# Attention on one core: half 0's scaling on VectorE, the sinks' exponentials in two instructions, weights' rests on GpSimd

## The chip, the core and the metric

The kernel runs on one core of one Trainium2 chip. The metric is the device time of one execution in microseconds; each kernel is run several times and the median counts. The engines are TensorE (PE; its weight loads are listed apart as PEld), VectorE (DVE), ScalarE (ACT), GpSimd (POOL) and SyncE (SP), which only issues transfers. Each engine takes its own instructions in the order in which they are written, and semaphores make it wait for the others.

## The reference

The reference is a two-layer decoder trunk in float32 with model width 1024, 512 positions and batch 1. Layer 0 is a gated short convolution, layer 1 is sliding-window attention; each is followed by a SwiGLU of inner width 2816, and every part has an RMSNorm before it and one behind it. The change lies in the attention, whose core is:

```python
kk, vv = with_prev(k), with_prev(v)          # each block of 128 keys with the block before it
scores = einsum('bnqhgd,bnkhd->bnhgqk', qb, kk) * scale
scores = where(valid, scores, NEG)           # window of 128 positions
sink = broadcast_to(sinks, ...)              # one extra logit per head
probs = softmax(concatenate([scores, sink], -1), -1)[..., :-1]
out = einsum('bnhgqk,bnkhd->bnqhgd', probs, vv)
attn = out.reshape(b, s, 1024) @ w_o
```

There are 16 query heads of width 64, 4 heads of keys and values, 4 blocks of 128 positions, and a rotation (rope) of 16 of each head's 64 columns. A head's sink only adds exp(sink − maximum) to the denominator of its softmax.

## The kernel before, in words

**Precision.** Every product of float32 matrices is made of three matmuls on split operands: a high part (the value rounded to the fast format `fp32r`) and a rest (value less high part), multiplied high by rest, high by high and rest by high. So each weight tile that is loaded (`raw`) is first split: ScalarE copies it to `whi`, then VectorE subtracts `wlo = raw - whi`. `split_weights` does this (lines 175 to 190), in one piece of 1024 columns (lines 188 and 189) or, with `slots=True`, in two of 512 (lines 182 and 183).

**The attention loop.** Lines 1542 to 1601 walk ten passes i = 0 to 9. In each they go through the string `ORDER` (lines 47 to 49) token by token, and each token writes the instructions of one step. A round works on one pair of heads (t = i, eight pairs); a token with "-" and the tokens T, P, L, W, O and o work on the pair of the pass before. Since every engine takes its instructions as written, `ORDER` fixes each engine's queue. The steps, each a method of `Heads`, `Queries` or `Early`:

- S: scores on TensorE (line 1334) into the banks `psc`. Half 0 holds the blocks 0 and 1, half 1 the blocks 2 and 3. M: masking and (negated) row maxima `nm` on VectorE (line 1346).
- E: exponentials on ScalarE with their row sums `rs` (line 1361), in four steps, E00 to E11: half, block. Behind the second step of each half stand two small activations for the sinks' exponentials `se` of this half (line 1368), one per head, of two columns.
- N: N0 adds `se` and `rs` (line 1374), takes the reciprocal `rd` (line 1376), both on VectorE, and scales half 0's exponentials on ScalarE, four activations (line 1381); N1 scales half 1's on VectorE, four operations (line 1384). The first block of the sequence has no block before it, so half 0's first piece has 128 columns and the other pieces have 256.
- T: the scaled exponentials are transposed on TensorE into a bank `pt` (line 1396), T0 to T3 by blocks of keys. P and L: the transpose is split, high part `phi` on ScalarE (line 1409), rest `plo` on VectorE (line 1413). W: TensorE weighs the values with both into `po` (line 1422). T2 and T3 use the banks of T0 and T1, so they wait for L0 and L1.
- O: the two halves of the heads' sums are joined, by a copy on ScalarE (line 1431) and an addition on VectorE (line 1433). o: the joined output is split for the output product (lines 1441 and 1442).
- Q, R, H: the queries two pairs ahead are projected on TensorE, rotated (VectorE lines 1261 and 1263, GpSimd lines 1267 and 1270) and split (ScalarE line 1280, then their rest on GpSimd, line 1281, tile `rhl`); the scores of the next round need `rhl`.
- G: weights: in passes 0 to 4 the query weights of the pair three ahead are split, from pass 5 on four tiles of output weights (`rest_w`, j = 0 to 3). g: output weights that are needed early (`early_w`), j = 0 and 1 in pass 4, j = 2 and 3 in pass 6.
- Z (also written Y) and z: parts of the output product that can already be made, in the later rounds.

GpSimd has another task: the SwiGLU weights are combined into sums in memory by transfers that accumulate, and GpSimd's queue issues them (line 547), in every pass behind its steps R and H.

The engines' queues depend on one another in a circle: N needs the exponentials, those need the scores, and those need the queries' split; T needs N.

Of the kernel before, what the change touches and what calls it, by code (L numbers as in the profile page):

```python
# [10 lines left out]
F32 = mybir.dt.float32  # L11
# [33 lines left out]

EARLY_IN, REST_IN = 2, 0
ORDER = (
    "R- S0 T0 T1 Q0 M0 O- Q1 Z0 P0 P1 S1 T2 T3 L0 o- Y0 Q2 L1 G M1 E00 E01 k H- g0 Q3 P2 P3 E10 E11 Z1 z0 W0 L2 L3 A A A N0 W1 W2 N1 W3 g1 z1"
)
NEXT = (0,)  # L50
STEP = {
    "S": "scores", "M": "maxima", "E": "exponents", "N": "normalise", "T": "turn", "P": "high",
    "L": "low", "W": "weigh", "O": "join", "o": "out", "Q": "project", "R": "rotate", "H": "split",
    "G": "weights", "Z": "project", "z": "out",
}
N_SLOT, N_WIDE, N_RAW, N_W = 35, 18, 7, 4
BOTH = 4
# [17 lines left out]
def yoco_kernel(  # L75
# [96 lines left out]
            h = at[1].start // S  # L172
            return self.of[h][:, at[1].start - h * S : at[1].stop - h * S]

    def split_weights(src, raw=None, slots=False):
        if raw is None:
            raw = fetch(src)
        if slots:
            hi, lo = Two("whi", F32R), Two("wlo", F32R)
            for h in range(2):  # L180
                c = slice(h * S, (h + 1) * S)
                nc.scalar.activation(hi[:, c], raw[:, c], AF.Copy)
                nc.vector.tensor_tensor(out=lo[:, c], in0=raw[:, c], in1=hi[:, c].bitcast(F32),
                                        op=ALU.subtract)
# [3 lines left out]
        nc.scalar.activation(hi, raw, AF.Copy)  # L188
        nc.vector.tensor_tensor(out=lo, in0=raw, in1=hi.bitcast(F32), op=ALU.subtract)
        return hi, lo  # L190

    def mm3(out, whi, wlo, xhi, xlo, start, stop, **kw):
# [1092 lines left out]
    class Queries:  # L1285
# [21 lines left out]
    class Heads:  # L1307
# [29 lines left out]
        def maxima(self, half):  # L1337

            pss = self.pss[half]
            nm = small.tile([P, 2, 2], F32, tag="nm", name=name("nm"))  # L1340
            pe = [slot("s") for _ in range(2)]
            self.pe[half], self.nm[half] = pe, nm
            for i, cc in self.spans(half):
                for e in range(2):
                    h = 2 * self.t + e
                    nc.vector.tensor_tensor_reduce(
                        out=pe[e][:, cc], in0=pss[e][:, cc],
                        in1=mask[:, 256 - (cc.stop - cc.start) :],
                        scale=-0.125, scalar=nsnk[:, h : h + 1], op0=ALU.add, op1=ALU.min,
                        accum_out=nm[:, e, i : i + 1],  # L1350
                    )

        def exponents(self, half, i):
            pe, nm = self.pe[half], self.nm[half]
            if half == i == 0:
                self.sums = [small.tile([P, 2, 2, 2], F32, tag=s, name=name(s))
                             for s in ("se", "rs")]
            se, rs = (x[:, half] for x in self.sums)
            cc = self.spans(half)[i][1]
            for e in range(2):  # L1360
                nc.scalar.activation(
                    pe[e][:, cc], pe[e][:, cc], AF.Exp, bias=nm[:, e, i : i + 1],
                    scale=-1.0, accum_out=rs[:, e, i : i + 1],
                )
            if i == 1:
                for e in range(2):
                    h = 2 * self.t + e
                    nc.scalar.activation(se[:, e], nm[:, e], AF.Exp, bias=snk[:, h : h + 1])

        def normalise(self, half):  # L1370
            pe = self.pe[half]
            if half == 0:
                se, rs = self.sums
                nc.vector.tensor_tensor(out=se, in0=se, in1=rs, op=ALU.add)
                self.rd = small.tile([P, 2, 2, 2], F32, tag="rd", name=name("rd"))
                nc.vector.reciprocal(out=self.rd, in_=se)
            rd = self.rd[:, half]
            for i, cc in self.spans(half):
                for e in range(2):
                    if half == 0:  # L1380
                        nc.scalar.activation(pe[e][:, cc], pe[e][:, cc], AF.Copy,
                                             scale=rd[:, e, i : i + 1])
                        continue
                    nc.vector.tensor_scalar(
                        out=pe[e][:, cc], in0=pe[e][:, cc], scalar1=rd[:, e, i : i + 1],
                        scalar2=None, op0=ALU.mult,
                    )
# [154 lines left out]
    with tc.manual_schedule(engines=ALL):  # L1542
        sum_on("a0")
        for i in range(KT + 2):
# [9 lines left out]
            for c in order.split():  # L1554
# [21 lines left out]
                if op in "SMENTPLWOo":  # L1576
                    t -= op in "TPLWOo"
                    of = hp
                elif op in "QRH":
# [118 lines left out]
```

## Time and profile before

| | |
|---|---|
| median of 3 runs | 1028.84 us (1028.47 to 1029.13) |
| the profiled execution | 1030.66 us |
| its span, first to last instruction | 1028.9 us |
| mean granted TensorE clock | 0.997 of full speed |
| busy TensorE / its weight loads | 1007.9 us (98%) / 886.4 us (86%) |
| busy VectorE | 868.9 us (84%) |
| busy ScalarE | 601.9 us (58%) |
| busy GpSimd | 189.6 us (18%) |
| read from HBM | 237.15 MB |

The page of the profile gives the busy time, the span in 40 slices and the groups of instructions; the trace behind it answers for any stretch. A row of a timeline has the start, the duration, the engine, the line, the operation and its tiles (out<-in, partitions x elements), how many like it follow each other without a break, and in square brackets the idle time of the engine ahead of it with what ended it. A row of a list of waits has the engine's instruction, what it waited for, the sum of these waits in us, their number and the mean. A row of a table by windows has the window, its length, and the busy time with the count of instructions of PE, PEld, VectorE, ScalarE and GpSimd, then the granted clock, the share of the transfers' engines and GB/s. A row of a group ends in: busy us, mean ns of one | idle time before them, and what ended most of it.

### The profile page before, as it was taken

To read this page: it belongs to the slowest core of one execution; us is meant where nothing else is said; L and a number is where in the kernel's file an instruction comes from. 1 tells how busy PE (TensorE), PEld (TensorE's weight loads), DVE (VectorE), ACT (ScalarE), POOL (GpSimd) and SP (SyncE) were. 2 spreads that over 40 slices of the span, in tenths; PEclk is the share of its full clock that TensorE was granted. 3 is DMA by queue.
4 is the path that set the end of the run, shared out by engine and by line. 5 is a ranking of instruction groups with operands and counts; after the bars stand their busy time and mean duration, and the time that the engine had idled before them with its cause. 6 is when DMAs were issued, how large, how long until landed. Compare 5 with 4: busy or idle time off the path is not lost. (4 is left out here: it accounts for less than half of the span.)

```text
span 1028.9 us, 16145 instructions
## 1 busy us (share of the span) xinstructions
PE 1007.9 (98%) x5944; PEld 886.4 (86%) x5944; DVE 868.9 (84%) x1448; ACT 601.9 (58%) x1083; POOL 189.6 (18%) x251
## 2 busy tenths in 40 slices
PE   9999999999999999999999989899999999999997
PEld 8888888999889898998897767689998998989986
DVE  5766767899779989989879887878997899899896
ACT  6323445866655464656577877968665563645641
POOL 0433033111111111100114553221211010111001
PEclk9999999999999999999999999999999999999999
DMA  9897689459969699779405887975899666988742
GB/s 357 284 268 223 182 255 351 132 169 292 349 220 301 202 306 339 217 232 327 146 22 155 202 264 172 279 259 146 249 295 324 176 253 210 289 299 255 256 165 82
DMA packets 66575, 244.50 MB, mean 238 GB/s; under 512 B 7872, under 2 KB 8384, under 8 KB 54720
## 3 DMA queue, kind: packets, MB, share of 16 engines
q1 hardware_dynamic: 51328, 145.98, 38.2%
q0 software_dynamic: 14592, 96.48, 37.2%
q8 instruction: 47, 0.77, 0.3%
q10 hardware_dynamic: 576, 1.02, 0.3%
q14 instruction: 32, 0.26, 0.1%
HBM read 237.15 MB, written 102.76 MB: 330 GB/s over the span
## 5 line engine op out<-in xcount | busy, mean ns | idle before, releaser
L479 DVE TENSOR_TENSOR wlo<-raw,whi 128x1024 fp32r<-128x1024 f32 x225 | 274.8, 1225 | 55.6 <-ACT whi L478 55.5
L478 ACT ACTIVATE whi<-raw 128x1024 fp32r<-128x1024 f32 x225 | 233.6, 1050 | 102.0 <-DVE raw L466 29.7
L1072 PE MATMUL gx<-xt,whi 128*128 128x512 f32 x480 | 120.4, 393 | 0.0
L1072 PEld LDWEIGHTS gx<-xt,whi 128*128 128x128 f32 x480 | 86.3, 189 | 15.5
L547 POOL DMA_DIRECT2D hsum<-in_w_gb_dram x96 | 62.5, 729 | 150.8 <-ACT whi L478 89.7
L1034 DVE TENSOR_TENSOR st<-gx,st 128x256 f32<-128x256 f32 x200 | 77.9, 419 | 2.5 <-ACT st L1050 0.4
L1050 ACT ACTIVATE st<-gx 128x256 f32<-128x256 f32 x120 | 43.3, 380 | 62.1 <-PE gx L1075 58.5
L547 POOL DMA_DIRECT2D hsum<-hsum x32 | 25.3, 790 | 293.1 <-ACT whi L478 201.8
L1075 PEld LDWEIGHTS gx<-xt,wlo 128*128 128x128 f32 x480 | 65.5, 190 | 4.7
L1075 PE MATMUL gx<-xt,wlo 128*128 128x256 f32 x480 | 66.9, 282 | 0.0
L1086 ACT ACTIVATE gr<-gr 128x1024 f32<-128x1024 f32 x20 | 21.3, 1063 | 49.9 <-DVE gr L1034 49.9
L193 PE MATMUL px<-wlo,ahi 128*128 128x512 f32 x120 | 46.8, 390 | 1.5 <-DVE mix L648 1.5
L195 PE MATMUL px<-whi,alo 128*128 128x512 f32 x120 | 46.7, 389 | 0.0
L194 PE MATMUL px<-whi,ahi 128*128 128x512 f32 x120 | 46.7, 389 | 0.0
L195 PE MATMUL gz<-xhi,wlo 128*128 128x256 f32 x160 | 45.5, 284 | 0.0
L193 PE MATMUL gz<-xt,whi 128*128 128x256 f32 x160 | 45.3, 283 | 0.0
L194 PE MATMUL gy<-xhi,whi 128*128 128x256 f32 x160 | 45.3, 283 | 0.0
L195 PE MATMUL gy<-xhi,wlo 128*128 128x256 f32 x160 | 45.3, 283 | 0.0
L193 PE MATMUL gy<-xlo,whi 128*128 128x256 f32 x160 | 45.3, 283 | 0.0
L194 PE MATMUL gz<-xt,whi 128*128 128x256 f32 x160 | 45.3, 283 | 0.0
L193 PE MATMUL gz<-xlo,whi 128*128 128x256 f32 x160 | 45.3, 283 | 0.0
L194 PE MATMUL gz<-xhi,whi 128*128 128x256 f32 x160 | 45.3, 283 | 0.0
(294 smaller groups left out, 2965.9 us busy)
## 6 DMA issues: line engine op xcount, KB each, us to landing
hsum<-in_w_gb_dram POOLq DMA_DIRECT2D x96, 512.0 KB, 7.5
raw<-hsum SPq DMA_DIRECT2D x88, 512.0 KB, 7.8
raw<-in_w_gb_dram SPq DMA_DIRECT2D x60, 512.0 KB, 6.6
hsum<-in_w_dn_dram POOLq DMA_DIRECT2D x36, 512.0 KB, 8.1
raw<-in_w_dn_dram SPq DMA_DIRECT2D x32, 512.0 KB, 5.8
hsum<-hsum POOLq DMA_DIRECT2D x28, 512.0 KB, 5.5
raw<-in_w_in_dram SPq DMA_DIRECT2D x21, 512.0 KB, 7.6
hsum<-in_w_dn_dram POOLq DMA_DIRECT2D x12, 768.0 KB, 10.6
```

The lines of the kernel that those rows point to most:

```text
L193: nc.tensor.matmul(out, whi, xlo, start=start, stop=False, **kw)
L194: nc.tensor.matmul(out, whi, xhi, start=False, stop=False, **kw)
L195: nc.tensor.matmul(out, wlo, xhi, start=False, stop=stop, **kw)
L478: self.begun = nc.scalar.activation(hi[:, :n], raw, AF.Copy)
L479: nc.vector.tensor_tensor(out=lo[:, :n], in0=raw, in1=hi[:, :n].bitcast(F32), op=ALU.subtract)
L547: nc.gpsimd.dma_start(dst, src, max_dma_last_dim=4 * 4 * S, **kw))
L1034: nc.vector.tensor_tensor(out=out, in0=a, in1=b, op=ALU.add)
L1050: nc.scalar.activation(ste, a, AF.Copy)
L1072: nc.tensor.matmul(banks[c][e], whi[:, kk], factors[p][k][2], start=opened and k == 0, stop=False, **kw)
L1075: nc.tensor.matmul(banks[c][e][:, :256], wlo[:, kk], factors[p][k][0], start=False, stop=k == 3 and p == 4, **kw)
L1086: nc.scalar.activation(kept[2], kept[2], AF.Silu)
```

## The change

The change has three parts, and the instructions of TensorE and SyncE keep their order.

1. **Half 0's scaling.** N0's four scalings go from ScalarE to VectorE, where they stand ahead of half 1's four.
2. **The sinks' exponentials.** The two pairs of activations of two columns become one pair of four columns, in a step `C` ("powers") of its own behind E11. For that the maxima of both halves share one tile, `nm` of [128, 2, 2, 2], and `se` and `rd` are laid out head by head.
3. **Rests on GpSimd.** `split_weights` can name the engine of the subtraction. The rests of the query weights of pairs 3 to 7, of the early output weights j = 2 and 3 and of the later ones j = 0, 1 and 2 go to GpSimd, each as two subtractions of 512 columns. The early ones j = 0 and 1 and the later one j = 3 stay on VectorE.

In sum VectorE gets 32 scalings and loses 5 subtractions of 1024 columns and 10 of 512; ScalarE loses 32 scalings and 16 of 32 small exponentials; GpSimd gets 20 subtractions of 512 columns.

VectorE in round 3, from the output's split to the rotation; `plo_6156` and `lp_5534` are the steps L2 and L3, `wlo_6174` is the rest of query weights, `s_6178` and `s_6179` are half 1's exponentials of the two heads. Before:

```order
L1442 TENSOR_TENSOR ohl_6161<-o_6123,ohl_6161 128x512
L1413 TENSOR_TENSOR plo_6108<-pt_6102,phi_6107 128x512
L189 TENSOR_TENSOR wlo_6174<-raw_6171,whi_6173 128x1024
L1346 ISA s_6178,nm_6177<-psc_6136,mask,nsnk 128x256
...
L1413 TENSOR_TENSOR plo_6156<-pt_6150,phi_6155 128x512
L1413 TENSOR_TENSOR lp_5534<-pt_6157,lp_5533 128x2x128
L1374 TENSOR_TENSOR se_6184<-se_6184,rs_6185 128x8
L1376 RECIPROCAL rd_6224<-se_6184 128x8
L1384 TENSOR_SCALAR s_6178<-s_6178,rd_6224 128x256
L1384 TENSOR_SCALAR s_6179<-s_6179,rd_6224 128x256
...
L1261 STREAM_SHUFFLE sh_6246<-pq_6109 128x512
```

And after, where `s_6111` and `s_6112` are half 0's exponentials:

```order
L1447 TENSOR_TENSOR ohl_6155<-o_6117,ohl_6155 128x512
L1418 TENSOR_TENSOR plo_6102<-pt_6096,phi_6101 128x512
L1352 ISA s_6172,nm_6110<-psc_6130,mask,nsnk 128x256
...
L1418 TENSOR_TENSOR plo_6150<-pt_6144,phi_6149 128x512
L1418 TENSOR_TENSOR lp_5534<-pt_6151,lp_5533 128x2x128
L1382 TENSOR_TENSOR se_6204<-se_6204,rs_6178 128x8
L1385 RECIPROCAL rd_6216<-se_6204 128x8
L1389 TENSOR_SCALAR s_6111<-s_6111,rd_6216 128x128
L1389 TENSOR_SCALAR s_6112<-s_6112,rd_6216 128x128
L1389 TENSOR_SCALAR s_6111<-s_6111,rd_6216 128x256
L1389 TENSOR_SCALAR s_6112<-s_6112,rd_6216 128x256
L1389 TENSOR_SCALAR s_6172<-s_6172,rd_6216 128x256
```

The subtraction of the query weights is gone from between L1 and the maxima of half 1, and half 0's four scalings stand between the reciprocal and half 1's.

GpSimd at the same place, from the rotation of one pair's queries to the transfers behind the split. Before:

```order
L1267 TENSOR_TENSOR sh_6074<-sh_6074,stab_5216 128x512
L1270 TENSOR_TENSOR ra_6076<-ra_6076,sh_6074 128x512
L547 DMA hsum_179<-hsum_178 64x2048
L1281 TENSOR_TENSOR rlo_6193<-ra_5578,rhi_6192 128x512
L1281 TENSOR_TENSOR rhl_6196<-ra_6076,rhl_6196 128x512
L547 DMA hsum_182<-in_w_gb_dram 64x2048
```

And after:

```order
L1270 TENSOR_TENSOR sh_6068<-sh_6068,stab_5216 128x512
L1273 TENSOR_TENSOR ra_6070<-ra_6070,sh_6068 128x512
L550 DMA hsum_179<-hsum_178 64x2048
L191 TENSOR_TENSOR wlo_6168<-raw_6165,whi_6167 128x512 x2
L1284 TENSOR_TENSOR rlo_6184<-ra_5578,rhi_6183 128x512
L1284 TENSOR_TENSOR rhl_6187<-ra_6070,rhl_6187 128x512
L550 DMA hsum_182<-in_w_gb_dram 64x2048
```

The two subtractions stand ahead of the queries' own rest (`rhl_6187`) and of the transfers that follow it. The row of `rlo_6184`, the keys' second half, is in this round alone.

VectorE in round 6, from L1 to the scaling of half 1; `wlo_6726` and `wlo_6727` belong to the later output weights (G), `wlo_6756` and `wlo_6757` to the early ones (g). Before:

```order
L1413 TENSOR_TENSOR plo_6664<-pt_6658,phi_6663 128x512
L183 TENSOR_TENSOR wlo_6726<-raw_6722,whi_6724 128x512
L183 TENSOR_TENSOR wlo_6727<-raw_6722,whi_6725 128x512
L1346 ISA s_6733,nm_6732<-psc_6692,mask,nsnk 128x256
...
L183 TENSOR_TENSOR wlo_6756<-raw_6752,whi_6754 128x512
L183 TENSOR_TENSOR wlo_6757<-raw_6752,whi_6755 128x512
L1413 TENSOR_TENSOR plo_6712<-pt_6706,phi_6711 128x512
L1413 TENSOR_TENSOR lp_5534<-pt_6713,lp_5533 128x2x128
L1374 TENSOR_TENSOR se_6739<-se_6739,rs_6740 128x8
```

And after:

```order
L1418 TENSOR_TENSOR plo_6651<-pt_6645,phi_6650 128x512
L1352 ISA s_6719,nm_6652<-psc_6679,mask,nsnk 128x256
...
L1418 TENSOR_TENSOR plo_6699<-pt_6693,phi_6698 128x512
L1418 TENSOR_TENSOR lp_5534<-pt_6700,lp_5533 128x2x128
L1382 TENSOR_TENSOR se_6751<-se_6751,rs_6725 128x8
```

Four subtractions of 512 columns are gone ahead of L2. The diff, cut to its core:

```diff
-    ... "Q3 P2 P3 E10 E11 Z1 z0 W0 L2 L3 A A A N0 W1 W2 N1 W3 g1 z1"
+    ... "Q3 P2 P3 E10 E11 C Z1 z0 W0 L2 L3 A A A N0 W1 W2 N1 W3 g1 z1"
-    def split_weights(src, raw=None, slots=False):
+    def split_weights(src, raw=None, slots=False, eng=nc.vector):
...
-        nc.vector.tensor_tensor(out=lo, in0=raw, in1=hi.bitcast(F32), op=ALU.subtract)
+        for c in ((0, D),) if eng is nc.vector else ((0, S), (S, D)):
+            c = slice(*c)
+            eng.tensor_tensor(out=lo[:, c], in0=raw[:, c], in1=hi[:, c].bitcast(F32),
+                              op=ALU.subtract)
...
         def weights(self):
-            self.w = split_weights(w_q[self.t])
+            self.raw = fetch(w_q[self.t])
+            self.w = split_weights(None, self.raw, eng=nc.gpsimd if self.t > LEAD else nc.vector)
...
-            if i == 1:
-                for e in range(2):
-                    h = 2 * self.t + e
-                    nc.scalar.activation(se[:, e], nm[:, e], AF.Exp, bias=snk[:, h : h + 1])
+
+        def powers(self):
+            self.se = small.tile([P, 2, 4], F32, tag="se", name=name("se"))
+            nm = self.nms.rearrange("p e a b -> p e (a b)")
+            for e in range(2):
+                h = 2 * self.t + e
+                nc.scalar.activation(self.se[:, e], nm[:, e], AF.Exp, bias=snk[:, h : h + 1])
...
             for i, cc in self.spans(half):
                 for e in range(2):
-                    if half == 0:
-                        nc.scalar.activation(pe[e][:, cc], pe[e][:, cc], AF.Copy,
-                                             scale=rd[:, e, i : i + 1])
-                        continue
                     nc.vector.tensor_scalar(
...
-                        early_w.append(split_weights(w_o[j // 2, j % 2], slots=j >= EARLY_IN))
+                        early_w.append(split_weights(w_o[j // 2, j % 2], slots=j >= EARLY_IN,
+                                                     eng=nc.gpsimd if j >= 2 else nc.vector))
...
-                        rest_w.append(split_weights(w_o[j // 2, 2 + j % 2], slots=j >= REST_IN))
+                        rest_w.append(split_weights(w_o[j // 2, 2 + j % 2], slots=j >= REST_IN,
+                                                    eng=nc.vector if j == 3 else nc.gpsimd))
```

More of the change, by code (lines that the diff above doesn't have):

```diff
@@ L1339, in maxima @@
             pss = self.pss[half]
[L1340 removed]
+            if half == 0:
+                self.nms = small.tile([P, 2, 2, 2], F32, tag="nm", name=name("nm"))
+            nm = self.nms[:, :, half]
             pe = [slot("s") for _ in range(2)]
@@ L1355, in exponents @@
             if half == i == 0:
-                self.sums = [small.tile([P, 2, 2, 2], F32, tag=s, name=name(s))
-                             for s in ("se", "rs")]
-            se, rs = (x[:, half] for x in self.sums)
+                self.rs = small.tile([P, 2, 2, 2], F32, tag="rs", name=name("rs"))
+            rs = self.rs[:, :, half]
             cc = self.spans(half)[i][1]
```

18 lines of the change are left out of this document (9 added, 9 removed), and 1 row of the table STEP.

## The prediction

> **What bounds the kernel now.** I read the busy shares, then windows by stage (length; busy time of TensorE, its weight loads, VectorE, ScalarE, GpSimd), then TensorE's waits inside the attention, then each engine's timeline there. Round i is pass i of the loop over `ORDER` (0 to 8); N(i) is the start of round i's sum of denominators on VectorE (line 1374).
>
> ```profile
> 548.00:680.00 132.00, 120.34 (x735) 96.56 (x734) 107.39 (x288) 104.23 (x293) 56.25 (x64) 0.99 0.83 233
> 680.00:1028.90 348.90, 342.11 (x2113) 308.64 (x2111) 309.20 (x474) 198.74 (x317) 41.34 (x61) 1.00 0.72 228
> PE pt L1396 <- DVE plo L1413: 4.7, 7, 1.0
> PE pt L1396 <- ACT s L1381: 4.1, 10, 0.8
> PE po L1422 <- DVE plo L1413: 1.9, 2, 0.9
> PE psc L1334 <- DVE nm L1346: 0.9, 1, 0.9
> ```
>
> The attention holds 132 − 120.34 = 11.66 us without a matmul, and four waits make 11.6 of them. All are for VectorE or ScalarE; the scaling that the change moves ends 4.1. Behind 680 TensorE is full but for the last slice of the page, so what TensorE gains or loses by 680 should arrive whole at the end.
>
> Round 3, from N(2) to N(3), shows the circle that times the middle rounds:
>
> ```profile
> 580.66 0.17 DVE L1374 TENSOR_TENSOR se<-se,rs 128x8 f32<-128x8 f32 x1 [1.52 <-ACT se L1368]
> 581.11 1.14 DVE L1384 TENSOR_SCALAR s<-s,rd 128x256 f32<-128x256 f32 x4
> 582.17 0.73 DVE L1261 STREAM_SHUFFLE sh<-pq 128x512 f32<-128x512 f32 x1
> 584.74 1.41 DVE L1433 TENSOR_TENSOR o<-po,o 64x512 f32<-64x512 f32 x2
> ...
> 581.16 1.49 ACT L1381 ACTIVATE s<-s,rd 128x128 f32<-128x128 f32 x4 [0.53 <-DVE rd L1376]
> 586.17 0.63 ACT L1441 ACTIVATE ohl<-o 128x512 fp32r<-128x512 f32 x1 [1.17 <-DVE o L1433]
> 589.41 0.46 ACT L1368 ACTIVATE se<-nm,snk 128x2 f32<-128x2 f32 x2
> 589.79 0.61 ACT L1280 ACTIVATE rhi<-ra 128x512 fp32r<-128x512 f32 x1
> 594.05 0.17 DVE L1374 TENSOR_TENSOR se<-se,rs 128x8 f32<-128x8 f32 x1 [1.59 <-ACT se L1368]
> ```
>
> VectorE leads for 586.17 − 580.66 = 5.51 us, down to the heads' sum (line 1433); then ScalarE runs for 7.88 without a gap until the sinks' exponentials release N(3). 5.51 + 7.88 = 13.39 is the round. TensorE follows this circle: it waits in it, at T0 and at T3.
>
> **The change part by part.** *First half's scaling to VectorE.* On ScalarE it takes 1.49 us, but ScalarE waits 1.17 behind it anyway; its removal gives this circle nothing. On VectorE it lies in the leading part. Four scalings of 256 columns start at 581.11 and the next operation at 582.17: 0.267 each. Half 0 has two of 256 and two of 128 columns: 2 × 0.267 + 2 × 0.133 = 0.80 us, taking half the time for half the columns. From above, four single ones bound it, from the group's mean:
>
> ```profile
> L1384 DVE TENSOR_SCALAR s<-s,rd 128x256 f32<-128x256 f32 x32 | 9.1, 350 | 0.3
> L1368 ACT ACTIVATE se<-nm,snk 128x2 f32<-128x2 f32 x32 | 7.5, 283 | 0.0
> ```
>
> 4 × 0.35 = 1.40, so 0.80 to 1.40; I take 0.80, since the same four run back to back today. The Trainium skill, "VectorE: DVE Perf Modes", section "The perf-mode tier table", has float32 tensor_scalar from SBUF at twice the speed of tensor_tensor; by it half 0 would be an estimated 0.4 us. The rows say 0.267 for 256 columns, 1.04 ns a column.
>
> *Sinks' exponentials.* The pair behind the first exponents goes: 589.79 − 589.41 = 0.38 us off ScalarE's part. The pair that stays is four wide instead of two; 283 ns for two columns is nearly all fixed, and I take no change.
>
> The circle: 5.51 + 0.80 + 7.88 − 0.38 = 13.81, that is +0.42. Rounds 2, 3 and 4 have this form: 3 × 0.42 = +1.26.
>
> *Queries' rests to GpSimd.* On VectorE they stand behind L1 and ahead of M1, and E1 waits for ScalarE, not for M1; taking them out gives the circle nothing. On GpSimd each is two of 512 columns ahead of the queries' own low part (`rhl`), for which the next round's S0 on TensorE waits. The same operation there:
>
> ```profile
> L1281 POOL TENSOR_TENSOR rhl<-ra,rhl 128x512 fp32r<-128x512 f32 x7 | 9.1, 1299 | 20.1 <-ACT rhl L1280 20.1
> 554.29 1.31 POOL L1281 TENSOR_TENSOR rhl<-ra,rhl 128x512 fp32r<-128x512 f32 x1
> 556.92 0.39 PE L1334 MATMUL psc<-rlo,rhl 64*128 64x256 f32 x2
> 577.63 1.30 POOL L1281 TENSOR_TENSOR rhl<-ra,rhl 128x512 fp32r<-128x512 f32 x1 [4.07 <-ACT rhl L1280]
> 603.86 1.30 POOL L1281 TENSOR_TENSOR rhl<-ra,rhl 128x512 fp32r<-128x512 f32 x1 [2.71 <-ACT rhl L1280]
> 558.20 0.33 PE L1396 MATMUL pt<-ident,s 128*128 128x128 f32 x1 [0.31 <-ACT s L1381]
> 558.89 1.17 PE L1396 MATMUL pt<-ident,s 128*128 128x128 f32 x7 [0.36 <-ACT s L1381]
> ```
>
> Two take 2.5 to 2.6 us. In rounds 2 to 4 GpSimd idles 2.71 to 4.07 us just there: hidden, barely in round 4. Round 0 has no gap: `rhl` moves from 554.29 to 556.8 and ends at 558.1, so S0 starts there instead of at 556.92, 1.2 late. The waits of 0.31 and 0.36 at T0 and T1 behind it take part of that, and the next round's waits at the same two places more; I take +0.2. The sums' DMAs queued behind the rests on GpSimd go out as much later; what they make is loaded in the FFN. So N(4) comes 0.2 + 1.26 = about 1.5 us later.
>
> *Late rests to GpSimd, and ScalarE's queue behind the exponents.* From N(4) on both pay:
>
> ```profile
> 609.75 1.04 ACT L188 ACTIVATE whi<-raw 128x1024 fp32r<-128x1024 f32 x1
> 610.82 1.23 DVE L189 TENSOR_TENSOR wlo<-raw,whi 128x1024 fp32r<-128x1024 f32 x1 [1.39 <-ACT whi L188]
> 641.14 0.51 PE L1422 MATMUL po<-plo,vt 128*128 128x256 f32 x2 [0.92 <-DVE plo L1413]
> 638.57 1.92 DVE L183 TENSOR_TENSOR wlo<-raw,whi 128x512 fp32r<-128x512 f32 x2
> 644.66 1.29 DVE L183 TENSOR_TENSOR wlo<-raw,whi 128x512 fp32r<-128x512 f32 x2 [0.96 <-ACT whi L182]
> 649.41 0.66 PE L1396 MATMUL pt<-ident,s 128*128 128x128 f32 x4 [0.84 <-DVE plo L1413]
> 650.67 0.44 PE L1396 MATMUL pt<-ident,s 128*128 128x128 f32 x2 [0.61 <-DVE plo L1413]
> 656.54 0.33 PE L1396 MATMUL pt<-ident,s 128*128 128x128 f32 x1 [0.49 <-ACT s L1381]
> 657.23 1.16 PE L1396 MATMUL pt<-ident,s 128*128 128x128 f32 x7 [0.36 <-ACT s L1381]
> 658.70 1.41 DVE L1433 TENSOR_TENSOR o<-po,o 64x512 f32<-64x512 f32 x2 [1.54 <-ACT o L1431]
> 662.30 0.44 PE L1396 MATMUL pt<-ident,s 128*128 128x128 f32 x2 [0.69 <-DVE plo L1413]
> ```
>
> TensorE's lateness against before, mark by mark. Round 5: the high part (609.75) no longer stands behind the scaling, so VectorE's wait of 1.39 goes, less the 0.80: 1.5 + 0.80 − 1.39 = +0.9. From there to 640 TensorE waits for nothing and carries it. Round 6: the 0.92 wait was behind a rest of 1.92 on VectorE that is gone: 0.0. Round 7: VectorE is freed of 0.96 + 1.29, pays 0.80, and starts its round some 0.5 later; T2 and T3 come about 0.9 sooner, of 0.84 + 0.61 waited: −0.8. Round 8: T0 and T1 need no ScalarE; 0.49 + 0.36 becomes about 0.1: −1.5. There too the wait of 1.54 for ScalarE goes, and 0.69 at T3 becomes about 0.25: −1.95.
>
> *What GpSimd's passes cost VectorE.* The trace has it in round 0:
>
> ```profile
> 551.95 1.29 POOL L1270 TENSOR_TENSOR ra<-ra,sh 128x512 f32<-128x512 f32 x1
> 552.33 1.99 DVE L189 TENSOR_TENSOR wlo<-raw,whi 128x1024 fp32r<-128x1024 f32 x1
> ```
>
> Beside a GpSimd pass this operation takes 1.99 instead of 1.23: up to 0.76 for a VectorE operation with two SBUF inputs. In the new order only line 1442 (heads' low part) can meet a rest, in rounds 5 to 7, for part of its length: 0 to 0.4, and only round 5's is carried on. I take +0.2.
>
> Sum: −1.95 + 0.2 = −1.75 us. The profiled execution took 1030.66 (span 1028.9 and 1.76 around it); it becomes 1028.9. The runs' median is 1028.84, 1.82 under the profiled one; I take the same difference from it: 1027.1 us. Own bounds: 1.40 for half 0 is +0.6 in rounds 2 to 4, +1.8 in all; if instead T0's and T1's shorter waits give back all of the 1.26, it is −1.3: 1025.8 to 1028.9.
>
> **The rivals.** *A, GpSimd becomes the bound (slower).* Each rest stands ahead of `rhl`, and with it S0, M0 and the circle. It decides where the rests outlast the gap ahead of `rhl`: 2.55 against 2.71 in round 4. If a pass stretches as VectorE's did (1.99 / 1.23 = 1.6), two take 4.1, and rounds 2 to 6 lose about 1.1 each: 5 × 1.1 − 1.75 = +3.75, 1032.6. Against it: the seven passes of line 1281 have a mean of 1.299, whatever ran beside them.
>
> *B, the late gains do not come.* The +0.9 stands at round 5, and in rounds 6 to 8 the waits of the same TensorE instructions stay with another releaser (L2 behind ScalarE's phi, T1 behind VectorE's eight scalings in one queue). Then about +0.9: 1029.7. For it: every gain there rests on one engine's queue being freed while the other keeps pace.
>
> *C, the slow clock goes.*
>
> ```profile
> 618.00:619.00 1.00, 1.00 (x4) 0.90 (x5) 1.00 (x2) 1.00 (x6) 0.00 (x0) 0.50 0.89 225
> 619.00:620.00 1.00, 1.00 (x4) 0.81 (x3) 1.00 (x6) 1.00 (x5) 0.00 (x0) 0.50 1.08 221
> 620.00:621.00 1.00, 1.00 (x3) 0.76 (x3) 0.94 (x5) 1.00 (x4) 0.62 (x1) 0.53 0.98 205
> ```
>
> Behind round 5's waits the granted clock is half for some 3 us: 1.5 us of work lost where TensorE is the bound. The change leaves waits of about 2.4 us there, as before, so I keep it; without it, 1025.6. The Trainium skill, "TensorE: Matmul & The Clock Gate", section "Why this matters for your kernels", asks for no idle gap over about 3 us. The trace differs: no wait of TensorE here is over 1.0 us.
>
> *D, half 0 at twice the speed*, as the mechanism of this kernel: 0.40 instead of 0.80 makes the circle 13.41, the three rounds cost nothing: −3.0, 1025.8. Against it, the 0.267 us per scaling of today. That rule is the Trainium skill's, "VectorE: DVE Perf Modes", named above.
>
> **How the numbers follow.** Forecast 0.50, A 0.10, B 0.20, C 0.15, D 0.05. A measurement of this kernel can tell about 0.2%, 2.06 us: faster is under 1026.8, slower over 1030.9. The forecast's own 1025.8 to 1028.9 gives 0.18 faster and 0.32 same; C and D give 0.19 faster and 0.01 same; B gives 0.18 same and 0.02 slower; A 0.10 slower. Faster 0.37, same 0.51, slower 0.12. The range leaves out A, the far side of C and of B: 1025.2 to 1030.2.
>
> **What the profile after would show.** Right: N to N in rounds 2 to 4 longer by 0.4; waits at T0 gone, waits at T2 and T3 of rounds 2 to 5 longer, ended by VectorE's line for `plo`; no wait of S0 for GpSimd but in round 1; rounds 6 to 8 without the 0.92, 0.84 and 0.69. Wrong: S0 waiting for `rhl` in each round (A); waits of the old size in rounds 6 to 8 (B); clock 1.00 throughout (C); scalings starting 0.13 us apart (D).

## The result, and the profile after

The changed kernel takes 1032.88 us (median of 6 runs, 1032.67 to 1033.90), the kernel before 1028.65 us in the same comparison (6 runs, 1027.83 to 1030.36). The ratio is 1.0041 with a 95% interval of 1.0028 to 1.0054: about 4.2 us slower, where 1.7 us faster was forecast and the range ended at 1030.2.

The two profiled executions differ ahead of the attention as well: that of before had a wait of 1.5 us in an earlier stage that no other profile here has. So positions are counted from a mark that all kernels share, TensorE's first matmul with the keys' projection of the `xlo` rows. Of before, then of after:

```profile
519.54 0.28 PE L193 MATMUL pk<-xlo,whi 128*128 128x256 f32 x1
```

```profile
517.21 0.28 PE L196 MATMUL pk<-xlo,whi 128*128 128x256 f32 x1
```

From the mark to the end of the span it is 1028.9 − 519.54 = 509.36 us before and 1030.9 − 517.21 = 513.69 after: 4.33 us, all of the loss. Below, "lateness" is always a position of this kind less that of before.

The window of the attention (length; busy TensorE, weight loads, VectorE, ScalarE, GpSimd; clock, transfers, GB/s) and TensorE's waits in it, after:

```profile
548.00:680.00 132.00, 117.75 (x712) 94.97 (x709) 105.11 (x298) 88.44 (x242) 80.54 (x83) 0.97 0.81 219
```

```profile
PE pt L1401 <- DVE plo L1418: 6.8, 9, 1.0
PE pt L1401 <- DVE s L1389: 4.7, 4, 2.5
PE psc L1338 <- DVE nm L1352: 0.8, 1, 0.8
PE po L1427 <- DVE plo L1418: 0.8, 1, 0.8
PE psc L1338 <- POOL rhl L1284: 0.7, 1, 0.7
```

GpSimd's busy time rose from 56.25 to 80.54 us and ScalarE's fell from 104.23 to 88.44, as the change says. VectorE's fell as well in this window, by 2.3 us, and yet TensorE now waits for VectorE almost alone. For GpSimd it waits once, 0.7 us. The granted clock fell from 0.99 to 0.97.

VectorE's sums of denominators (line 1382) and the group of eight scalings (line 1389, which the timeline names by its first form), in the order of the rounds, after:

```profile
553.99 1.81 DVE L1382 TENSOR_TENSOR se<-se,rs 128x8 f32<-128x8 f32 x1 [2.26 <-ACT se L1376]
556.07 2.08 DVE L1389 TENSOR_SCALAR s<-s,rd 128x128 f32<-128x128 f32 x8
565.91 2.34 DVE L1382 TENSOR_TENSOR se<-se,rs 128x8 f32<-128x8 f32 x1 [1.11 <-ACT se L1376]
581.50 0.17 DVE L1382 TENSOR_TENSOR se<-se,rs 128x8 f32<-128x8 f32 x1 [1.52 <-ACT se L1376]
595.45 0.17 DVE L1382 TENSOR_TENSOR se<-se,rs 128x8 f32<-128x8 f32 x1 [1.59 <-ACT se L1376]
609.82 0.17 DVE L1382 TENSOR_TENSOR se<-se,rs 128x8 f32<-128x8 f32 x1 [0.47 <-ACT se L1376]
624.45 0.17 DVE L1382 TENSOR_TENSOR se<-se,rs 128x8 f32<-128x8 f32 x1 [1.59 <-ACT se L1376]
643.39 0.79 DVE L1382 TENSOR_TENSOR se<-se,rs 128x8 f32<-128x8 f32 x1 [1.52 <-ACT se L1376]
644.45 4.20 DVE L1389 TENSOR_SCALAR s<-s,rd 128x128 f32<-128x128 f32 x8
658.24 0.16 DVE L1382 TENSOR_TENSOR se<-se,rs 128x8 f32<-128x8 f32 x1
```

An addition of eight columns takes 0.17 us in rounds 2 to 5 and 7, and 1.81, 2.34 and 0.79 in rounds 0, 1 and 6. The eight scalings take 2.08 in round 0 and 4.20 in round 6. No idle time is shown for these: a stalled instruction looks like a long one. What lies beside them on GpSimd, after:

```profile
554.51 1.26 POOL L1284 TENSOR_TENSOR rhl<-ra,rhl 128x512 fp32r<-128x512 f32 x1
565.11 1.87 POOL L1284 TENSOR_TENSOR rhl<-ra,rhl 128x512 fp32r<-128x512 f32 x1
566.36 1.86 POOL L1270 TENSOR_TENSOR sh<-sh,stab 128x512 f32<-128x512 f32 x1
641.62 2.52 POOL L183 TENSOR_TENSOR wlo<-raw,whi 128x512 fp32r<-128x512 f32 x2
644.44 2.49 POOL L183 TENSOR_TENSOR wlo<-raw,whi 128x512 fp32r<-128x512 f32 x2 [0.29 <-ACT whi L182]
```

The ends agree each time. Round 0: the addition ends at 553.99 + 1.81 = 555.80, the pass at 555.77. Round 1: 568.25 and 568.22. Round 6: 644.18 and 644.14; then the scalings meet the next two passes. In rounds 0 and 1 the addition waits for two passes in a row, and the ones that end last are not the moved rests but passes that GpSimd made before the change too (`rhl` and the next rotation, `sh`); the two rests ahead of them in GpSimd's queue have pushed them back beside the sum. In round 6 they are the moved rests themselves. Taken one by one, the first two of the eight, of 128 columns, last 1.333 and 1.300 us beside passes of some 1.25, and the other six the usual 0.35.

VectorE's operations with an input in PSUM keep their length beside a pass, as one of the maxima and one of the rests from PSUM show (all maxima of 256 columns here last 0.47 to 0.49 us), after:

```profile
562.60 3.13 POOL L191 TENSOR_TENSOR wlo<-raw,whi 128x512 fp32r<-128x512 f32 x2
563.78 0.69 DVE L1418 TENSOR_TENSOR plo<-pt,phi 128x512 fp32r<-128x512 f32 x1
603.54 2.54 POOL L191 TENSOR_TENSOR wlo<-raw,whi 128x512 fp32r<-128x512 f32 x2
604.56 0.48 DVE L1352 CUSTOM_DVE_ANT_0 s<-psc,mask,nsnk 128x256 f32<-128x256 f32 x1
```

TensorE in round 6, and the clock behind it, after:

```profile
645.93 0.30 PE L1401 MATMUL pt<-ident,s 128*128 128x128 f32 x1 [2.45 <-DVE s L1389]
647.32 1.76 PE L1401 MATMUL pt<-ident,s 128*128 128x128 f32 x7 [1.09 <-DVE s L1389]
```

```profile
647.00:648.00 1.00, 0.68 (x3) 0.68 (x4) 1.00 (x6) 0.00 (x0) 1.00 (x2) 0.50 0.61 225
649.00:650.00 1.00, 1.00 (x4) 0.81 (x3) 1.00 (x7) 0.60 (x1) 0.00 (x0) 0.50 1.41 369
```

TensorE waits 3.5 us for the two stalled scalings, and a second stretch of half clock follows, which before did not have.

### The profile page after: what moved, and what is told of

Its sections match the earlier page's. It is cut to its first block, busy times and chain, and to the rows that moved or that the text cites. A ratio compares the mean times of both kernels' runs of the same rounds, so it can differ in the third digit from the quotient of the medians.

```text
span 1030.9 us, 16136 instructions
## 1 busy us (share of the span) xinstructions
PE 1008.8 (98%) x5944; PEld 887.7 (86%) x5944; DVE 870.3 (84%) x1465; ACT 587.9 (57%) x1035; POOL 215.0 (21%) x271
## 3 DMA queue, kind: packets, MB, share of 16 engines
q10 hardware_dynamic: 576, 1.02, 0.3%
## 5 line engine op out<-in xcount | busy, mean ns | idle before, releaser
L198 PE MATMUL gz<-xt,wlo 128*128 128x256 f32 x160 | 45.3, 283 | 0.0
```

Of the source, the lines that this page charges most:

```text
L198: nc.tensor.matmul(out, wlo, xhi, start=False, stop=stop, **kw)
```

## The experiments

**Theories.** L (lock): a VectorE operation whose inputs all lie in SBUF stands still while a GpSimd pass runs. The rests that moved to GpSimd lie beside the sums and scalings of rounds 0, 1 and 6, or push other passes beside them, and stall them. The Trainium skill, "SBUF — State Buffer", section "Who interferes with whom", states such a rule: a VectorE instruction with two SBUF inputs contends with a GpSimd instruction that reads SBUF, and so can `tensor_scalar` in a two-port mode; whoever is first keeps the ports for its whole instruction. S: the eight scalings on VectorE are the loss themselves. Q: GpSimd's longer queue delays the queries' rest and so the scores (rival A).

In the table, "to the end" is the distance from the mark to the end of the span against 509.36 us, and the two columns before it are the lateness of rounds 4 and 6 at the start of their sums of denominators, all from one profile each; the median stands beside that of the kernel before in the same comparison. The profiled execution of a run lies up to 0.9 us from the run's median (half0_act 1028.73 against 1029.63), so differences of that size in the last three number columns are not safe.

| run | median, us | before | ratio (95%) | round 4 | round 6 | to the end |
|---|---|---|---|---|---|---|
| changed kernel | 1032.88 | 1028.65 | 1.0041 (1.0028 to 1.0054) | +4.30 | +3.60 | +4.33 |
| early_queries_vec | 1030.86 | 1028.83 | 1.0021 (1.0012 to 1.0030) | +1.46 | +0.73 | +1.62 |
| late_pair_vec | 1030.88 | 1028.83 | 1.0016 (1.0007 to 1.0025) | +4.23 | +1.93 | +2.19 |
| both_vec | 1028.23 | 1028.83 | 0.9994 (0.9985 to 1.0002) | +1.45 | +0.77 | −0.53 |
| half0_act | 1029.63 | 1028.83 | 1.0007 (0.9998 to 1.0015) | +0.56 | +0.15 | +0.43 |
| only_half0 | 1030.62 | 1028.83 | 1.0011 (1.0003 to 1.0020) | +2.57 | +2.07 | +1.08 |
| only_powers | 1027.30 | 1028.83 | 0.9984 (0.9976 to 0.9993) | −1.11 | −1.75 | −2.07 |
| passes_that_read | 1031.79 | 1028.83 | 1.0030 (1.0017 to 1.0042) | +2.84 | +3.81 | +3.88 |
| passes_that_write | 1029.60 | 1028.83 | 1.0009 (0.9999 to 1.0019) | +0.67 | +0.92 | +1.01 |
| half0_late4 | 1026.13 | 1030.06 | 0.9966 (0.9952 to 0.9980) | −1.02 | −3.31 | −3.00 |
| half0_late5 | 1026.86 | 1030.06 | 0.9971 (0.9961 to 0.9981) | −1.01 | −1.59 | −2.86 |
| late4_sooner | 1023.24 | 1030.06 | 0.9939 (0.9926 to 0.9951) | −1.04 | −2.63 | −5.12 |
| powers_sooner | 1024.69 | 1030.06 | 0.9952 (0.9939 to 0.9964) | −1.05 | −1.45 | −3.65 |

**Rests of rounds 0 and 1 back on VectorE** (changed kernel):

```diff
-            self.w = split_weights(None, self.raw, eng=nc.gpsimd if self.t > LEAD else nc.vector)
+            self.w = split_weights(None, self.raw, eng=nc.gpsimd if self.t > LEAD + 2 else nc.vector)
```

> The changed kernel with the query weights' rests of pairs 3 and 4 (rounds 0 and 1) back on VectorE; pairs 5 to 7 stay on GpSimd. Theory L (lock): VectorE's operations whose inputs lie all in SBUF, the sum of denominators and the scalings, stand still until GpSimd's passes beside them are over; in the changed kernel that made the sum 1.81 instead of 0.17 us in round 0 and 2.34 in round 1. With the rests of these two rounds gone from GpSimd both are 0.17 again, round 4 comes about 2.5 us sooner, and the time is 1030.0 to 1030.8 (changed kernel 1032.9). Rival S (the scalings themselves are the loss: eight take 1.98 us a round instead of 1.06 for four): nothing changes, 1032.5 to 1033.2. Rival Q (GpSimd's queue delays the queries' rest and so the scores): only the one wait of the scores for GpSimd of 0.69 us goes, 1032.2.

Measured 1030.86. The sums of rounds 0 and 1, then round 6 with its scalings:

```profile
555.73 0.17 DVE L1382 TENSOR_TENSOR se<-se,rs 128x8 f32<-128x8 f32 x1 [1.31 <-ACT se L1376]
566.08 0.17 DVE L1382 TENSOR_TENSOR se<-se,rs 128x8 f32<-128x8 f32 x1 [0.38 <-ACT se L1376]
...
641.33 0.79 DVE L1382 TENSOR_TENSOR se<-se,rs 128x8 f32<-128x8 f32 x1 [1.52 <-ACT se L1376]
642.39 4.20 DVE L1389 TENSOR_SCALAR s<-s,rd 128x128 f32<-128x128 f32 x8
```

Rounds 0 and 1 are at 0.17 again, round 4 comes 4.30 − 1.46 = 2.84 us sooner, and 4.33 − 1.62 = 2.71 of it arrive at the end. Round 6 is locked as in the changed kernel. L holds, though the median is 0.06 us above its range; S expected nothing and Q 0.7.

**Rests of round 6's early output weights back on VectorE** (changed kernel):

```diff
                         early_w.append(split_weights(w_o[j // 2, j % 2], slots=j >= EARLY_IN,
-                                                     eng=nc.gpsimd if j >= 2 else nc.vector))
+                                                     eng=nc.vector))
```

> The changed kernel with the rests of the early output weights j = 2 and 3 (round 6) back on VectorE; all else as changed. L: round 6's sum of denominators (0.79 us) and its eight scalings (4.20 us) are 0.17 and 2.0 again, the waits of 2.45 and 1.09 us of TensorE for them go, and with them the second stretch of half clock (3.2 us, 1.6 us of work); some of the waits of before at these places (0.92, 0.84, 0.61) come back: 1029.5 to 1031.0. S and Q: VectorE gets 2.6 us of work back in round 6 and GpSimd loses no wait of the scores there: 1032.9 to 1034.

Measured 1030.88, 2.14 us sooner to the end:

```profile
642.16 0.17 DVE L1382 TENSOR_TENSOR se<-se,rs 128x8 f32<-128x8 f32 x1 [0.71 <-ACT se L1376]
642.60 2.06 DVE L1389 TENSOR_SCALAR s<-s,rd 128x128 f32<-128x128 f32 x8
```

The same VectorE that got 2.6 us of work back is done sooner, because its other work no longer stalls. The clock did not do what L expected. The second stretch of half clock (from 646.8 us on in the changed kernel) does not go but comes later, at 651.6 us. What goes is the first one, of 619.5 us; in its place stands one at 590.1 us, behind which round 4 is no later than in the changed kernel (+4.23 against +4.30).

**Both edits in one.**

> Both edits of the two runs before in one: rests of rounds 0, 1 and of j = 2, 3 on VectorE; on GpSimd stay the queries' of rounds 2 to 4 and the later output weights' j = 0 to 2. L: no sum of denominators over 0.2 us and no scaling group over 2.1; the two gains add up: 1027.0 to 1028.7, that is no slower than before the change (1028.65). S: 1032.5 to 1034. Q: 1032.2.

Measured 1028.23. By the profiles the gains add: 2.71 + 2.14 = 4.85, and 4.33 + 0.53 = 4.86 are measured. By the medians it is 2.02 + 2.00 = 4.02 against 4.65, so the agreement to 0.01 us is luck. What is left of the change, with half 0's scaling on VectorE throughout, is within 0.2% of before. The locks, with the clock that follows them, make more than the whole net loss.

**Half 0's scaling on ScalarE again** (changed kernel, rests as in the change):

```diff
                 for e in range(2):
+                    if half == 0:
+                        nc.scalar.activation(pe[e][:, cc], pe[e][:, cc], AF.Copy,
+                                             scale=rd[:, e, i : i + 1])
+                        continue
                     nc.vector.tensor_scalar(
```

> The changed kernel with half 0's scalings on ScalarE again, all rests as in the change. L: the sums of denominators of rounds 0, 1 and 6 still wait for GpSimd (1.6, 2.2 and 0.6 us over 0.17), so half or more of the loss stays; of the rest goes 0.9 us a round in rounds 2 to 4 less what ScalarE's queue takes back (0.5 a round), and in round 6 T0 waits no more for locked scalings (2.1 us, and the clock's 1.6): 1029.5 to 1031.5. S: the loss is the scalings, so the time comes back to before's or under it: 1027.5 to 1028.7. Q: nothing but the waits at T0 changes, 1032.

Measured 1029.63. The sums stay locked in rounds 0, 1 and 6 (1.81, 1.08 and 0.78 us), so this removes only what lay on half 0: 3.25 us by the medians, 3.9 by the profiles. L's range held at its lower end, but not its reason that half or more of the loss stays: 0.8 of 4.2 us stays. The run alone does not refute S; the next two do.

**The scaling alone, and the two instructions alone** (each on the kernel before; the first deletes the branch above, the second has the change's step `C` and shared tiles):

> The kernel before with half 0's scaling on VectorE and nothing else of the change: all rests on VectorE, sinks' exponentials in four instructions. L: no pass of GpSimd lies beside a sum of denominators or a scaling, so no lock; the leading part of the circle in rounds 2 to 4 is 0.9 us longer (eight scalings take 1.98 us where four took 1.06) and nothing is taken off ScalarE's part: 3 x 0.9 = 2.7, less what TensorE's waits at T0 and T1 for the scaling on ScalarE give back in the later rounds (0.5 to 0.9): 1030.5 to 1031.5 (before 1028.8). S: the scaling makes the whole of the change's loss, 1032.5 to 1033.

> The kernel before with the sinks' exponentials in two instructions behind the last exponents, and nothing else of the change. L: ScalarE's part of the circle in rounds 2 to 4 is 0.38 us a round shorter, as the changed kernel has it: 3 x 0.38 = 1.1 us, of which TensorE keeps most: 1027.5 to 1028.2. S: the same. Q: the same; the run measures the part that the forecast put at 0.38 a round.

Measured 1030.62 and 1027.30, the second 0.2 us under L's range. The scaling alone costs 1.8 us by the medians and 1.1 by the ratio and the profile, not 4.2. From round 2's sum to round 3's, before has 13.39 us; with the scaling alone it is 594.32 − 580.01, with the two instructions alone 591.77 − 578.76:

```profile
580.01 0.17 DVE L1374 TENSOR_TENSOR se<-se,rs 128x8 f32<-128x8 f32 x1 [1.52 <-ACT se L1368]
594.32 0.17 DVE L1374 TENSOR_TENSOR se<-se,rs 128x8 f32<-128x8 f32 x1 [1.58 <-ACT se L1368]
```

```profile
578.76 0.17 DVE L1383 TENSOR_TENSOR se<-se,rs 128x8 f32<-128x8 f32 x1 [1.34 <-ACT se L1377]
591.77 0.17 DVE L1383 TENSOR_TENSOR se<-se,rs 128x8 f32<-128x8 f32 x1 [1.59 <-ACT se L1377]
```

That is 14.31 and 13.01: +0.92 and −0.38, where the forecast had +0.80 and −0.38. The two instructions alone, one of the change's three parts, make a kernel 1.5 us faster than before.

half0_act and only_powers differ in the rests' engine alone. So the rests on GpSimd cost 1029.63 − 1027.30 = 2.33 us with half 0 on ScalarE. One by one the three parts make 1.79 − 1.53 + 2.33 = 2.59 us; the other 1.64 of the measured 4.23 (2.8 by the profiles) come only where half 0's scaling on VectorE and the rests on GpSimd are in one kernel, as round 6's stalled scalings of half 0 are.

**The lock by itself** (the kernel before with work of no use on GpSimd behind step H of rounds 2 to 4):

```diff
+                if op == "H" and i in (2, 3, 4):
+                    for _ in range(7):
+                        nc.gpsimd.tensor_tensor(out=spare, in0=stab[:, :192], in1=ctab[:, :192], op=ALU.subtract)
```

In the second kernel the loop holds `nc.gpsimd.memset(spare, 0.0)`, fourteen times.

> The kernel before with seven additional GpSimd subtractions of 192 columns (about 0.47 us each, 3.3 us in all) in rounds 2, 3 and 4 right behind the queries' rest; they read two tables in SBUF and write a tile that nobody reads, so that they lie beside these rounds' sums of denominators. L: the sums take up to 2 us instead of 0.17 and the scalings are drawn out to the passes' ends, in rounds 2 and 3 above all: 1032 to 1036. Q: GpSimd is only later with what is queued behind (the next rotation, the sums' transfers), for which it had 2 to 4 us of slack: 1028.5 to 1029.5, sums of 0.17.

> As the run before, with fourteen memsets of 192 columns in the place of the seven subtractions: GpSimd is as busy or busier, but reads nothing. [...] If the mere work of GpSimd were the cause (Q, or a slower SBUF), the time is that of the run before.

For the second kernel L expected, by the Trainium skill's rule named above, the sum of denominators at 0.17 us and a time of 1028.5 to 1031, with the scalings open. Measured 1031.79 and 1029.60. Round 2 in the first and in the second kernel, where four scalings of 256 columns took 1.14 us before:

```profile
578.18 4.65 POOL L1600 TENSOR_TENSOR spare<-stab,ctab 128x192 f32<-128x192 f32 x7
```

```profile
578.72 0.17 DVE L1375 TENSOR_TENSOR se<-se,rs 128x8 f32<-128x8 f32 x1 [1.51 <-ACT se L1369]
579.17 2.46 DVE L1385 TENSOR_SCALAR s<-s,rd 128x256 f32<-128x256 f32 x4
```

```profile
578.03 4.48 POOL L1600 MEMSET spare<- 128x192 f32 x14
```

```profile
578.59 0.17 DVE L1375 TENSOR_TENSOR se<-se,rs 128x8 f32<-128x8 f32 x1 [1.51 <-ACT se L1369]
579.03 1.39 DVE L1385 TENSOR_SCALAR s<-s,rd 128x256 f32<-128x256 f32 x4
```

GpSimd is busy about equally long beside the same operations, 4.65 and 4.48 us, but in passes of 0.60 us in the first kernel (0.47 was expected) and of 0.26 to 0.29 in the second. Where it reads SBUF the scalings take 2.46 us, where it only writes 1.39. That alone is not a difference between reading and writing: in both kernels a scaling waits for the pass beside it and ends 0.15 us behind it (0.75 us long in the first kernel, 0.42 in the second, 0.35 undisturbed), and the passes that only write are shorter. Beside one memset:

```profile
579.65 0.42 DVE L1385 TENSOR_SCALAR s<-s,rd 128x256 f32<-128x256 f32 x1
579.64 0.28 POOL L1600 MEMSET spare<- 128x192 f32 x1
```

For the scalings this agrees with what the Trainium skill, "SBUF — State Buffer", section "Who interferes with whom", says of `tensor_scalar` in a two-port mode. The wait arrives whole in the circle: from round 2's sum to round 3's the first kernel takes 593.42 − 578.72 = 14.70 us and the second 592.23 − 578.59 = 13.64 where before takes 13.39, so 1.31 and 0.25 more, as the scalings do (1.32 and 0.25). No half clock lies in that stretch in any of the three.

The same section's rule on reads (the Trainium skill, "SBUF — State Buffer") shows at a VectorE operation with two SBUF inputs, the subtraction of query weights in round 4, in the first and in the second kernel:

```profile
605.62 1.47 DVE L190 TENSOR_TENSOR wlo<-raw,whi 128x1024 fp32r<-128x1024 f32 x1 [0.49 <-ACT whi L189]
605.98 1.58 POOL L1600 TENSOR_TENSOR spare<-stab,ctab 128x192 f32<-128x192 f32 x1
```

```profile
603.32 1.78 DVE L190 TENSOR_TENSOR wlo<-raw,whi 128x1024 fp32r<-128x1024 f32 x1
604.27 0.89 POOL L1600 MEMSET spare<- 128x192 f32 x3
```

In both the subtraction first waits for the queries' rest (its end is at 606.02 and 604.01) and ends 1.08 and 1.09 us behind it. Then the pass that reads waits for the subtraction, 1.58 us instead of 0.60, while three memsets run beside it at their usual pace. And the reciprocal, which reads one tensor from SBUF and writes one there, keeps its 0.20 us beside a reading pass (578.93 in the pass from 578.86 to 579.46). So L as it was put is too wide: not every operation whose inputs lie in SBUF waits, but those with two inputs there, and the scalings.

L's number for the sum of denominators failed: it took 0.17 to 0.25 us in the first kernel, not up to 2. The passes are short; in rounds 3 and 4 the sum starts 0.37 and 0.40 us into one of 0.60 and ends 0.02 us behind it. Beside the memsets it kept 0.17 us, but they end too soon behind its start to tell a wait from none. The scalings paid instead: three of the four wait out a whole pass each. The time came a little under L's range, and Q's 1028.5 to 1029.5 is out: GpSimd's queue is about equally long in both kernels, and the second is only 0.8 us slower than before.

**Versions without the lock.** Half 0 on VectorE for the late pairs only (`if half == 0 and self.t < 4` in the branch above, or `< 5`), on the kernel with both edits:

> Two instructions for the sinks; half 0's scaling on VectorE only for pairs 4 to 7 (on ScalarE for 0 to 3); on GpSimd the queries' rests of rounds 2 to 4 and the later output weights' j = 0 to 2; the early ones j = 2 and 3 on VectorE. L: no lock is left, the circle of rounds 2 and 3 keeps the 0.38 us that the two instructions saved (round 4 came 1.11 us sooner with these alone), and from round 4 on the gain of the run with both edits comes on top (it came 1.45 late there and ended 0.53 ahead, 1.98 us): 1025.2 to 1026.3. S, by which scaling on VectorE only costs: 1027.3 or more, no better than the two instructions alone.

> As the run before, with half 0's scaling on VectorE for pairs 5 to 7 only. In round 4 the high part of the output weights stands behind the scaling on ScalarE again, and VectorE waits 1.4 us for it: of the 0.93 us that the change gains between rounds 4 and 5 some 0.6 goes: L 1025.8 to 1026.9.

And with the early output weights j = 2 and 3 split at the start of round 6, once on half0_late4 and once with all of half 0 on ScalarE and all query weights' rests on VectorE:

```diff
-    "R- S0 T0 T1 ...
+    "R- g2 g3 S0 T0 T1 ...
...
-                    u = 2 * (t - EARLY - 1) + n[0]
-                    if u in (-2, -1, 2, 3):
+                    u = 2 * (t - EARLY - 1) + n[0] % 2
+                    if u in ((2, 3) if n[0] > 1 else (-2, -1)):
```

> As half0_late4, with the early output weights j = 2 and 3 split at the start of round 6 instead of its middle and end: there VectorE stood idle for 4.2 us while TensorE had work. L: the waits that VectorE's four subtractions cause behind L1, L2 and ahead of round 7's maxima (0.5 to 0.9 us at two places) go: 1024.4 to 1025.6. If instead the loads or the slots are not there so soon, ScalarE and VectorE stand still behind them and it is 1026 or more.

> Two instructions for the sinks, all half 0's scalings on ScalarE, query weights' rests on VectorE, the later output weights' j = 0 to 2 on GpSimd, and j = 2 and 3 split at the start of round 6 on VectorE. Tells what the rests alone bring in the late rounds without the scaling: from the two instructions alone (1027.3) less the waits of 0.6 and 0.8 us for the rest in rounds 6 and 7: 1025.9 to 1026.8. If the late gain comes from the scaling alone: 1027.3.

All four beat both kernels: 1026.13, 1026.86, 1023.24 and 1024.69. The medians of half0_late4 and half0_late5 lie in their ranges; the other two are 1.2 us below theirs. The kernel before has a median of 1030.06 in this comparison, 1.2 above the other ones, so the ratios in the table say more than the absolute times. TensorE's waits from round 6 on in late4_sooner, and its window of the attention:

```profile
630.88 0.66 PE L1405 MATMUL pt<-ident,s 128*128 128x128 f32 x4 [0.65 <-DVE plo L1422]
632.14 0.44 PE L1405 MATMUL pt<-ident,s 128*128 128x128 f32 x2 [0.61 <-DVE plo L1422]
644.42 0.44 PE L1405 MATMUL pt<-ident,s 128*128 128x128 f32 x2 [0.61 <-DVE plo L1422]
649.84 1.48 PE L1405 MATMUL pt<-ident,s 128*128 128x128 f32 x8 [0.17 <-DVE s L1393]
654.83 0.44 PE L1405 MATMUL pt<-ident,s 128*128 128x128 f32 x2 [0.32 <-DVE plo L1422]
```

```profile
548.00:680.00 132.00, 123.36 (x756) 99.78 (x753) 108.63 (x301) 101.30 (x272) 73.73 (x79) 1.00 0.86 240
```

The waits of 0.92 and 0.84 us in rounds 6 and 7 of before are gone, two of 0.65 and 0.61 us have come in round 6, and the clock never falls in the attention. Between round 4 and the end the kernel gains 5.12 − 1.04 = 4.1 us, up to 1.7 of it the stretch of half clock that before has there. powers_sooner gains 3.65 − 1.05 = 2.6 there with all of half 0 on ScalarE, of which the two instructions alone bring 2.07 − 1.11 = 0.96; the rests' new places and engines bring the most. The 1.5 us between the two kernels are about the price of the one stretch of half clock that powers_sooner has, so what half 0's scaling on VectorE brings in the late rounds stays open.

## Why the prediction was wrong

The sign was wrong, because one term was missing.

- **The step that failed** is "What GpSimd's passes cost VectorE": "In the new order only line 1442 (heads' low part) can meet a rest, in rounds 5 to 7, for part of its length: 0 to 0.4 [...] I take +0.2." Line 1442 (1447 after) met nothing that cost it: it lasts 0.69 us in every round, before and after. The step left out the sums of denominators, which have two SBUF inputs, and the scalings, which go from SBUF to SBUF; and it looked for the rests alone, not for the passes that they push back in GpSimd's queue. Such passes met the sums of rounds 0 and 1, the rests themselves met round 6: 1.64, 2.17 and 0.62 us over 0.17 for the sums and about 2.1 for round 6's scalings. In place of +0.2, 4.9 us were measured (both_vec against the changed kernel, by the profiles; 4.65 by the medians), of which the second stretch of half clock is up to 1.7.
- **The row was there and was read wrongly.** 1.99 us instead of 1.23 was taken as a stretch of "up to 0.76". It was a wait for the pass to end: the subtraction ended at 552.33 + 1.99 = 554.32, 1.08 us behind the pass beside it, 0.15 less than its own length of 1.23; the sums, 0.17 long, end 0.03 behind a pass, 0.14 less. A wait has no fixed price; it is whatever is left of the pass, and of the next where that stands right behind it, whether the waiting operation has 1024 columns or 8.
- **The circle's sum held.** +0.42 a round was forecast and +0.54 is what the two parts alone make (+0.92 − 0.38). Round 4 was forecast 1.5 us late; with no lock ahead of it (early_queries_vec) it is 1.46. So close a match is luck: that kernel enters round 1's sum 0.20 ahead and then loses about 0.55 in each of three rounds.
- **The late gains came only in part.** From round 4 to the end the forecast gained 1.5 + 1.95 = 3.45. The changed kernel gained 0.94 up to round 5, where 0.6 was forecast, and lost it again: −0.03 in all. both_vec gained 1.98 with j = 2 and 3 back on VectorE, and late4_sooner 4.1, up to 1.7 of it the clock, with their split at another place.
- **Queries' rests ahead of the scores:** the scores wait for GpSimd once, 0.69 us in round 0, where 1.2 late was forecast; in the later rounds they are hidden, as forecast.
- **Rivals.** A's time (1032.6) came by luck, its mechanism did not: TensorE waits 0.7 us for GpSimd in all, not 1.1 in each of five rounds. B is half true: in round 6 the waits came back with another releaser, the locked scalings. C did not happen here, it went the other way; but its price of 1.5 us was of the right size: five executions of powers_sooner took 1023.07 us at a mean clock of 0.999, 1024.48 to 1024.87 at 0.996 and 0.997, and 1025.91 at 0.994. D's price is refuted: the eight scalings take 0.92 us more than four, not 0.4.

## What to carry to other kernels

Before work moves to GpSimd, list what will run beside each of its passes in the new order, the passes pushed back in its queue included, and mark VectorE's operations with two inputs in SBUF and its scalings from SBUF to SBUF; each of them can wait for a whole pass, however small it is, and the profile will show it as a long instruction with no idle time. Place GpSimd's passes beside VectorE work that reads PSUM, which kept its length here. And try each part of a combined change alone: here one of the three was a gain of 1.5 us by itself, and splitting the same weights at an idle place gained 2.9 us (half0_late4 to late4_sooner, up to 1.7 of it the clock).

## What the runs showed of the hardware that was not expected

- **The clock falls in whole steps.** In every profile here half clock in the attention comes in stretches of about 3.4 us, 1.7 us of full clock lost in each: none in late4_sooner, two in the changed kernel, early_queries_vec, late_pair_vec and half0_act, one and one of double length in passes_that_read, one in each of the others. The longest single wait of TensorE near them was mostly 1.0 us, and the same three waits (0.82, 1.0 and 0.61 us) in round 5 were followed by a drop in the changed kernel and not in half0_late4. The trace's clock records show that the changes lie on a grid of 3.413 us: between two stretches lie 23.89 us in the changed kernel, 58.03 in late_pair_vec and 10.24 in passes_that_read, that is 7, 17 and 3 steps. In all 14 profiles together the clock drops 18 times in the attention, each time behind a step in which TensorE was busy with matmuls for at most 0.61 of it. Each of the 8 such steps busy for under 0.52 was followed by a drop, those between were followed by one in some kernels and not in others (0.513 in the changed kernel, 0.525 in half0_late4, behind the three waits named). So what counts is how the waits fall into a step rather than how long the longest is; what decides between 0.52 and 0.61 stays open.
- **A scaling has a large fixed part.** Two of 256 and two of 128 columns cost 0.92 us more; with 0.265 for 256 (four in 1.06) that leaves 0.195 for 128. By these two points the 128 further columns cost 0.07 us, an estimate of 0.55 ns a column, and some 0.12 us are fixed. The forecast's 1.04 ns a column came from dividing the one by the other. So the fixed part spoils D's price, not its rate: by the same kind of estimate a subtraction costs 1.04 ns a column (1.22 us for 1024 columns, 0.69 for 512), about twice as much as a scaling.
- **Two queues take turns.** With passes of 0.60 us, started every 0.67 (seven in 4.65 us beside four scalings), one scaling gets done per pass; in rounds 0 and 1 of the changed kernel one addition waited for two passes in a row. What decides between the two was not tried.
